# Retention queries and keys in the Strassen form, and their T4 (with that of nine other units) made by an accumulating load

## The chip, the cores and the metric

The kernel runs on one core of a Trainium2 chip. The metric is the device time of one execution in microseconds, the median of three. The engines are named as the profile names them: PE is TensorE (matmuls), DVE is VectorE, ACT is ScalarE, POOL is GpSimd, and SP issues plain DMAs.

## The reference, cut to what matters

One decoder block on 512 tokens of width 1024, all in float32. Only the input projection and what hangs on it bears on this change.

```
h = rmsnorm(x, norm1_w);  proj = h @ w_in
rq, rk, rv, rg, mq, mk, mv, ga, gb = split(proj)      # widths 512 512 1024 1024 512 512 512 1024 1024
rq, rk = rotary(rq), rotary(rk) * 128**-0.5           # 4 heads of 128
ret = silu(rg) * groupnorm(retention(rq, rk, rv));  a = ret @ w_ret_out
b = moba_attention(rmsnorm(mq), rmsnorm(mk), mv) @ w_moba_out
x = x + (sigmoid(ga) * a + sigmoid(gb) * b) @ w_o
x = x + (silu(rmsnorm(x) @ w_gate) * (rmsnorm(x) @ w_up)) @ w_down
```

## The kernel before, in words

All weights lie in one DRAM array, `wall`, as chunks of 128x1024 floats (512 KB), in the order in which they are used. A float32 product is made of three float32r products: each weight chunk is split into a high half `wh` (a cast on ACT, L407) and a low half `wl` (a subtraction on DVE), and `mm3` runs high x high, high x low and low x high. So each 128x1024 piece costs a load, a cast on ACT and a subtraction on DVE. Every engine call recorded by the pacing helper has line 218, so tiles tell more than lines.

Work comes in units. A unit in the Strassen form (`wino_unit`) takes four weight quarters B11, B12, B21, B22 of one chunk each (a wide one takes two) and makes seven products of 24 matmuls of 256 columns: B11, T1, T2, B21, B22, T3, T4, where T1 is a sum of the stored chunks of B12 and B11, T3 of B22 and B12, T2 = T1 + B22 and T4 = T2 + B21 (the signs aside). T1 and T3 are made by loads alone: SP loads one chunk (L332), and GpSimd adds the other by an accumulating DMA (L334). T2 is made by DVE in place (`raw<-raw,raw`, 128x1024). T4 was made in the same way by DVE, except in wide units with two chunks to a quarter (`w_o`, most of `w_ffn_down`), where an accumulating DMA issued right behind T2's low half does it (L371). T4's product runs late: in a Strassen unit that follows, behind that unit's T1 product. A unit's results leave PSUM through `Quarters`: three ACT copies (a plain one at L859, two negated ones at L862 and L865) and two DVE subtractions of 128x512 into a tile `qb`, and then the unit's own work.

A unit in the plain feature form (`feat_blocks`) takes its weights as they are: four chunks, four pieces, 192 matmuls of 256 columns.

`ORDER` sets the units: mv, rg0, rk0, rv0, gb0, rk1, rv1, rg1, gb1, b0, b1, ga0, a0, ga1, a1, then w_o and the feed-forward part. (rg: retention gate, rk: retention queries and keys of two heads, rv: values, ga and gb: branch gates, a and b: branch outputs.) `WRQ` says whether rk0 and rk1 run in the Strassen form; before, they don't.

Between groups of matmuls a second stream runs from a list `bg`: one step per 24 matmuls in the feature form, one per 12 in the Strassen form. First come 38 attention steps (scores on PE; on DVE a row maximum `mx`, its scaled negative `nb`, a reciprocal `rl`, the scaling of `p`; on ACT the exponential `p` and copies `pt` out of PSUM), spread over rg0, rk0, rv0 and gb0, then retention scores, retention values with their statistics (`bs`, `mvs`), and the gate `qa<-qa,r_y,sg` in halves of 256 columns. rk's own results go through rotary on DVE: `rot`, three multiplications and an addition for each of four results, then a cast on ACT and a low half on DVE.

All eight PSUM banks and the 47 slots of 128x1024 in SBUF are shared by every kind of tile, so a new tile waits for the last reader of the slot it gets. Each engine runs its queue in the order in which the program wrote it; nothing overtakes.

The raw chunks in flight are limited: one that has been split frees its slot, and that issues the next load. At most three pieces, at times four, are split and not yet used up.

Of the kernel before, what the change touches and what calls it, by code (L numbers as in the profile page):

```python
# [40 lines left out]
OEXTRA = 5  # L41
FEXTRA = -2
ORDER = (("rg", 0), ("rk", 0), ("rv", 0), ("gb", 0), ("rk", 1), ("rv", 1), ("rg", 1), ("gb", 1), ("b", 0), ("b", 1), ("ga", 0), ("a", 0), ("ga", 1), ("a", 1))
WRQ = (0, 0)
RLAG = (1, 2, 3)
SLAG = (1, 1, 1)
ROT = 1
# [11 lines left out]
HLAG = 1  # L59
LLAG = 1  # L60
CHUNKS = (6, 6, 6, 4)
T4DMA = ("X2",)


K_ID, K_ONE, K_NEG, K_TRI, K_GM, K_GN, K_COS, K_SIN = 0, 128, 256, 384, 512, 528, 544, 1056
# [15 lines left out]
def weight_plan():  # L81
# [19 lines left out]
    def wino(name1, col1, name2, col2, order=NORMAL):  # L101
        quarters = ((name1, col1, 0), (name2, col2, 0), (name2, col2, 4), (name1, col1, 4))
        units.append(("W", [(n, (k0 + k) * P, c + i * P) for n, c, k0 in quarters for i in (0, 1) for k in range(4)],
                      order))
# [3 lines left out]
    def cols(col):  # L108
        units.append(("X", ("w_in", halves, col, 256), NORMAL))
# [3 lines left out]
    for name, i in ORDER:  # L113
        if name == "rg":
            cols(C_RG + 512 * i)
        elif name == "rv":
            cols(C_RV + 512 * i)
        elif name == "rk" and WRQ[i]:
            wino("w_in", C_RQ + 256 * i, "w_in", C_RK + 256 * i)
# [21 lines left out]
def quarter_parts(unit):  # L141

    if unit[0] == "W":
        return [1024]
    _, rows, _, half = unit[1]
    n = len(rows[0]) * half
    return [min(1024, n - i) for i in range(0, n, 1024)]


def unit_chunks(unit):  # L150
    return 4 * len(quarter_parts(unit)) if unit[0] in "WX" else 2
# [14 lines left out]
def hybrid_block(ctx: ExitStack, tc: tile.TileContext, wall, xin, xtok, n2, cin, out):  # L166
# [107 lines left out]
    chunk, chunk_of, width, t4dma = 0, {}, {}, set()  # L274
    for u, unit in enumerate(plan):
        chunk_of[u] = chunk
        if unit[0] in "WX":
            ws = quarter_parts(unit)
            order = unit[2].split()
            if f"{unit[0]}{len(ws)}" in T4DMA:  # L280
                t4dma.add(u)
            for j, n in enumerate(ws):
                for q in ("B11", "B21", "B22", "T1", "T2", "T3", "T4"):
                    width[u, (q, j)] = n
            if unit[2] == PLAIN:
                loads += [(u, (q, 0), [chunk + c]) for q, c in (("B11", 0), ("B21", 3), ("B12", 1), ("B22", 2))]
                porder += [(u, (q, 0)) for q in order]
                for q in order:
                    width[u, (q, 0)] = 1024
                chunk += 4  # L290
                continue
            for q, cs in WLOADN if order.index("T1") < order.index("B21") else WLOAD:
                loads += [(u, (q, j), [chunk + c * len(ws) + j for c in cs]) for j in range(len(ws))]
            rest = False
            for q in order:
                if q == "/":
                    rest = True
                elif q[0] == "*":
                    for _ in range(int(q[1:])):
                        porder += left.pop(0) if left else []  # L300
                else:
                    x = [(u, (q[:3].rstrip("w"), j)) for j in range(len(ws))]
                    if rest:
                        left.append(x)
                    else:
                        porder += x
        else:
            loads += [(u, i, [chunk + i]) for i in range(2)]
            porder += sum(left, [])
            left = []  # L310
            if u >= STARTERS:
                porder += [(u, i) for i in range(2)]
            for i in range(2):
                width[u, i] = 1024
        chunk += unit_chunks(unit)
# [217 lines left out]
    def two(x):  # L533
        return x.rearrange("p (u c) -> p u c", u=2)
# [78 lines left out]
    for k in range(KT):  # L613
        if k % 2 == 0:
            hf[k // 2] = big(f"hf{k}")
        f = two(hf[k // 2])[:, k % 2]
# [166 lines left out]
    def wino_unit(w, ev, hooks={}):  # L783

        u = cur[0]
        cur[0] += 1
        order = plan[u][2].split()
        wide = plan[u][0] == "X" and plan[u][1][3] == 512
        banks = {}

        def bank(b):
            if b not in banks:
                z = zbank if b == "Z" else main_ps()
                banks[b] = [z, main_ps()] if wide else z
            return banks[b]

        def third(x):
            ev.c22(x)
            if "T4w" in order:
                ev.u3(x)  # L800

        def first(x):
            ev.p1(*([x, bank("Z")] if seed else [x]))

        whole = "T4w" in order
        seed = not wide and order[1] != "B21"
        table = {"B11": ("X", "A11", True, False, first), "T1": ("Y", "S1", True, False, ev.p5),
                 "T2": ("X", "S2", False, False, ev.u2), "B21": ("Z", "A12", not seed, True, ev.c11),
                 "B22": ("Y", "S4", False, True, ev.c12), "T3": ("X", "S3", False, whole, third),
                 "T4": ("X", "A22", False, True, ev.c21),  # L810
                 "T4w": ("W", "A22", True, True, getattr(ev, "c21w", None))}

        def run(q):
            b, m, start, stop, out = table[q]
            wino_prod(w, u, bank(b), m, q.rstrip("w"), start, stop, out)

        rest = False
        for q in order:
            if q == "/":
                rest = True  # L820
            elif q[0] == "*":
                for _ in range(int(q[1:])):
                    wino_finish()
            elif rest:
                wpend.append(lambda q=q: run(q))
            else:
                run(q)
                if q in hooks:
                    hooks[q]()
# [310 lines left out]
    def rot_out(h0):  # L1140
        def f(r, c, x):

            a, b = halves(nm("rot"))
            hf = RDK // 2
            if h0 is None:
                c, h = c
                V.tensor_tensor(a, x, cosT, ALU.mult)
                V.tensor_tensor(b[:hf], x[hf:], sinT[hf:], ALU.mult)
                V.tensor_tensor(b[hf:], x[:hf], sinT[:hf], ALU.mult)
                V.tensor_tensor(a, a, b, ALU.add)  # L1150
                (rqT, rkT)[c][h] = split(f"r{c}_{h}", a, None, SLAG[1])
                return
            cos, sin = (y[:, r * 256:(r + 1) * 256].unsqueeze(1).to_broadcast([P, 2, 256]) for y in (cosT, sinT))
            V.tensor_tensor(two(a), two(x), cos, ALU.mult)
            V.tensor_tensor(two(b)[:hf], two(x)[hf:], sin[hf:], ALU.mult)
            V.tensor_tensor(two(b)[hf:], two(x)[:hf], sin[:hf], ALU.mult)
            V.tensor_tensor(a, a, b, ALU.add)
            if (c, h0) not in rT:
                H, L = big(f"rH{c}_{h0}", F32R), big(f"rL{c}_{h0}", F32R)
                rT[c, h0] = H, L  # L1160
                for i in (0, 1):
                    s = slice(i * 512, (i + 1) * 512)
                    (rqT, rkT)[c][h0 + i] = Two(H[:, s], L[:, s])
            H, L = (two(y)[:, :, r * 256:(r + 1) * 256] for y in rT[c, h0])
            later(ROT, lambda: A.copy(H, two(a)))
            later(ROT + 1, lambda: V.tensor_tensor(L, two(a), H.bitcast(F32), ALU.subtract))
        return f
# [141 lines left out]
    def rk_unit(n):  # L1309
        h = 2 * n  # L1310
        if WRQ[n]:
            wino_unit(hW, Quarters(rot_out(h)))
# [415 lines left out]
```

## Time and profile before

| | |
|---|---|
| median of three executions | 801.82 us (799.88 to 802.16) |
| the profiled execution | 800.78 us, of which the span of the trace is 798.7 us |
| PE busy | 782.8 us (98%) |
| DVE busy | 648.9 us (81%) |
| ACT busy | 439.8 us (55%) |
| granted clock of PE | 0.997 over the whole |

The span runs from the first to the last instruction. Busy PE counts time in which a matmul was under way; with 98% busy, nearly each microsecond less of matmul is a microsecond less of time, unless PE then waits for something else.

### The profile page before, as it was taken

To read this page: it belongs to the slowest core of one execution; us is meant where nothing else is said; L and a number is where in the kernel's file an instruction comes from. 1 tells how busy PE (TensorE), PEld (TensorE's weight loads), DVE (VectorE), ACT (ScalarE), POOL (GpSimd) and SP (SyncE) were. 2 spreads that over 40 slices of the span, in tenths; PEclk is the share of its full clock that TensorE was granted. 3 is DMA by queue.
4 is the path that set the end of the run, shared out by engine and by line. 5 is a ranking of instruction groups with operands and counts; after the bars stand their busy time and mean duration, and the time that the engine had idled before them with its cause. 6 is when DMAs were issued, how large, how long until landed. Compare 5 with 4: busy or idle time off the path is not lost.

```text
span 798.7 us, 13670 instructions
## 1 busy us (share of the span) xinstructions
PE 782.8 (98%) x5398; PEld 722.8 (90%) x5398; DVE 648.9 (81%) x978; ACT 439.8 (55%) x722; POOL 64.1 (8%) x84
## 2 busy tenths in 40 slices
PE   6999999999999999999999999999999999999998
PEld 5889998889899998998988798988999899988996
DVE  7789877977799588877578989879887978889877
ACT  8457764757337458653445565544555455645541
POOL 0004000000000000000001000011101110111000
PEclk9999999999999999999999999999999999999999
DMA  9843352334426547371799705579836893689502
GB/s 330 230 113 80 115 128 50 106 80 133 125 67 179 133 136 182 106 185 56 230 353 246 170 1 132 126 193 291 231 102 180 221 287 111 150 213 294 136 1 106
DMA packets 38080, 125.95 MB, mean 158 GB/s; under 512 B 4224, under 2 KB 4480, under 8 KB 38016
## 3 DMA queue, kind: packets, MB, share of 16 engines
q1 hardware_dynamic: 28800, 93.88, 33.8%
q0 software_dynamic: 9216, 31.20, 22.5%
q8 instruction: 42, 0.69, 0.3%
q14 instruction: 22, 0.18, 0.1%
HBM read 122.97 MB, written 2.10 MB: 157 GB/s over the span
## 4 chain that ended last, share of the span: by engine, by line
PE 84%; DVE 8%; ACT 4%; issue 2%; DMA 2%; POOL 0%; SPq 0%; DVEq 0%; ACTq 0%; POOLq 0%
PE pm L218 76%; PE ps L218 8%; DVE wl L218 2%; ACT wh L407 2%; DMA raw<-wall 2%; DVE xr L218 1%; DVE raw L218 1%; DVE ws L218 1%; DVE h L218 1%; DVE fb L218 1%; DVE gs L218 1%; DVE gsl L218 0%; ACT f L1508 0%; ACT h L1496 0%; DVE xn L218 0%
## 5 line engine op out<-in xcount | busy, mean ns | idle before, releaser
L218 DVE TENSOR_TENSOR wl<-raw,wh 128x1024 fp32r<-128x1024 f32 x203 | 245.1, 1220 | 44.7 <-ACT wh L407 34.7
L407 ACT CAST wh<-raw 128x1024 fp32r<-128x1024 f32 (+1 forms) x224 | 219.5, 1006 | 67.6 <-DVE raw L218 47.5
L218 PE MATMUL pm<-h,wh 128*128 128x256 f32 x1248 | 227.3, 285 | 3.3 <-ACT h L1496 1.3
L218 PEld LDWEIGHTS pm<-h,wh 128*128 128x128 f32 x1248 | 196.3, 193 | 4.8 <-ACT h L1496 1.5
L218 PE MATMUL pm<-h,wl 128*128 128x256 f32 x624 | 177.2, 284 | 0.0
L218 PEld LDWEIGHTS pm<-h,wl 128*128 128x128 f32 x624 | 120.5, 193 | 0.0
L334 POOL DMA_DIRECT2D raw<-wall x56 | 49.6, 898 | 633.3 <-DMA raw<-wall 153.3
L218 PE MATMUL pm<-hA,wh 128*128 128x256 f32 x448 | 83.2, 286 | 1.8 <-DVE qb L218 1.8
L218 PEld LDWEIGHTS pm<-hA,wh 128*128 128x128 f32 x448 | 70.1, 192 | 3.0 <-DVE qb L218 2.0
L218 PE MATMUL pm<-wh,hA 128*128 128x256 f32 (+1 forms) x304 | 69.1, 310 | 0.0
L218 PE MATMUL pm<-wh,hS 128*128 128x256 f32 x320 | 63.1, 287 | 0.4 <-ACT pm L859 0.4
L218 PE MATMUL pm<-hA,wl 128*128 128x256 f32 x224 | 63.4, 283 | 0.0
L218 DVE TENSOR_TENSOR raw<-raw,raw 128x1024 f32<-128x1024 f32 (+1 forms) x48 | 57.0, 1189 | 0.8
L218 PEld LDWEIGHTS pm<-wh,hA 128*128 128x128 f32 x304 | 51.0, 191 | 2.4
L218 PEld LDWEIGHTS pm<-wh,hS 128*128 128x128 f32 x320 | 51.7, 191 | 0.9 <-ACT pm L859 0.6
L218 DVE TENSOR_TENSOR xr<-xr,pm 128x512 f32<-128x512 f32 x74 | 47.1, 681 | 1.3 <-PE pm L218 1.3
L218 PE MATMUL pm<-hS,wh 128*128 128x256 f32 x256 | 47.4, 285 | 0.0
L218 PE MATMUL pm<-wl,hA 128*128 128x256 f32 (+1 forms) x152 | 46.5, 306 | 0.0
L218 PE MATMUL pm<-wl,hS 128*128 128x256 f32 x160 | 45.3, 283 | 0.0
L218 PEld LDWEIGHTS pm<-hA,wl 128*128 128x128 f32 x224 | 42.8, 191 | 0.0
L218 PE MATMUL pm<-wh,gsh 128*128 128x512 f32 x112 | 39.9, 391 | 0.2
L218 PEld LDWEIGHTS pm<-hS,wh 128*128 128x128 f32 x256 | 40.0, 192 | 0.1
(254 smaller groups left out, 1397.9 us busy)
## 6 DMA issues: line engine op xcount, KB each, us to landing
raw<-wall SPq DMA_DIRECT2D x153, 512.0 KB, 4.6
raw<-wall POOLq DMA_DIRECT2D x55, 512.0 KB, 6.9
raw<-wall SPq DMA_DIRECT2D x23, 256.0 KB, 4.8
raw<-wall POOLq DMA_DIRECT2D x9, 256.0 KB, 6.7
xr<-xtok SPq DMA_DIRECT2D x4, 512.0 KB, 7.7
out<-xr SPq DMA_DIRECT2D x8, 256.0 KB, 2.1
x<-xin SPq DMA_DIRECT2D x7, 256.0 KB, 5.4
cs<-cin SPq DMA_DIRECT2D x1, 512.0 KB, 5.5
```

Of the source, the lines that this page charges most:

```text
L218: return f(out, *args, **kw)
L334: nc.gpsimd.dma_start(t[:, s], wall[c, :, s], accum_op=ALU.add)
L407: A.copy(h, src)
```

## The change

Three edits go together. `WRQ = (1, 1)` puts rk0 and rk1 into the Strassen form: 168 matmuls of 256 columns each instead of 192, seven pieces to cast and split instead of four, a T2 sum on DVE, three copies on ACT and two subtractions on DVE to take the quarters out of PSUM, and 14 steps of the second stream instead of 10 (both with the two of the T4 product that runs inside the unit). `T4CHUNKS = 52` makes T4 by an accumulating load wherever the unit's first chunk is below 52: in mv, rg0, rk0, rv0, gb0, rk1, rv1, rg1, gb1 and ga0. In the eight of these that were in the Strassen form before, a DVE sum of 128x1024 goes and a GpSimd DMA comes. The wide units keep theirs, so the rest of the program has its old order.

```
-WRQ = (0, 0)
+WRQ = (1, 1)
...
-T4DMA = ("X2",)
+T4CHUNKS = 52
...
         if unit[0] in "WX":
             ws = quarter_parts(unit)
             order = unit[2].split()
-            if f"{unit[0]}{len(ws)}" in T4DMA:
+            if len(ws) > 1 or chunk < T4CHUNKS:
                 t4dma.add(u)
```

In the built program PE has 5310 matmuls instead of 5358, GpSimd issues 14 more DMAs (four for T1 and T3 of the two rk units, ten for T4), SP two more. From ga0's T4 on, every engine has the same order as before.

Place one, VectorE at the end of rk0. Before: the T2 sum of rv0 (`raw_1162`), one rotary group, attention, and T2's low half.

```order
L218 TENSOR_REDUCE mx<-ps_1617 128x2
L218 SCALAR_TENSOR_TENSOR nb<-mx,qs 128x2
L218 RECIPROCAL rl<-l 128x2
L218 TENSOR_SCALAR p_1628<-p_1628,rl 128x128 x2
L218 TENSOR_TENSOR raw_1162<-raw_1162,raw_1246 128x1024
L218 TENSOR_TENSOR r_1_1631<-rot_1590,r_1_1631 128x512
L218 TENSOR_TENSOR rot_1683<-pm_1577,cs 128x512
L218 TENSOR_TENSOR rot_1683<-pm_1577,cs 64x512 x2
L218 TENSOR_TENSOR rot_1683<-rot_1683 128x512
L218 TENSOR_REDUCE mx<-ps_1697 128x2
L218 SCALAR_TENSOR_TENSOR nb<-mx,qs 128x2
L218 TENSOR_TENSOR wl_1725<-raw_1162,wh_1688 128x1024
```

Now, at the place where PE stands before the transposes of `p_1746` (T4's product of rk0 is half done):

```order
L218 TENSOR_TENSOR rL_0_1678<-rot_1672,rH_0_1677 128x2x256
L218 RECIPROCAL rl<-l 128x1
L218 TENSOR_SCALAR p_1692<-p_1692,rl 128x384
L218 TENSOR_TENSOR rot_1764<-qb_1214,cs 128x512
L218 TENSOR_TENSOR rot_1764<-qb_1214,cs 64x512 x2
L218 TENSOR_TENSOR rot_1764<-rot_1764 128x512
L218 TENSOR_TENSOR raw_1358<-raw_1358,raw_1437 128x1024
L218 TENSOR_REDUCE mx<-ps_1770 128x1
L218 SCALAR_TENSOR_TENSOR nb<-mx,qs 128x1
L218 RECIPROCAL rl<-l 128x1
L218 TENSOR_SCALAR p_1746<-p_1746,rl 128x512
```

Two of the three rotary groups ahead of this place now read `qb`, which a DVE subtraction made, and rv0's T2 sum has moved to between the last of them and the maximum of `ps_1770`, with a whole attention step behind it.

ScalarE at the same place. Before: exponentials with one cast between them.

```order
L1035 ACTIVATE p_1856,l<-ps_1845,nb,qs 128x512
L407 CAST wh_1873<-raw_1400 128x1024
L1035 ACTIVATE p_1886,l<-ps_1875,nb,qs 128x512
L865 ACTIVATE qb_1669<-pm_1670 128x512
L1067 COPY pt_1763<-ps_1907 128x2x128
L1072 COPY pt_1765<-ps_1907 128x128
```

Now: behind the exponential of `ps_1770` stand the cast of a rotary result, the copy that seeds a bank of rv0, the cast of rv0's T2, and only then the copies that free the bank `ps_1802`.

```order
L1035 ACTIVATE p_1781,l<-ps_1770,nb,qs 128x512
L1165 CAST rH_0_1677<-rot_1764 128x2x256
L859 COPY pm_218<-pm_1707 128x512
L407 CAST wh_1800<-raw_1358 128x1024
L1067 COPY pt_1642<-ps_1802 128x2x128
L1072 COPY pt_1644<-ps_1802 128x128
```

PE's next scores, `ps_1876`, take the bank that `ps_1802` leaves, so they have moved behind all six of these rows.

Place two, VectorE from rk1 to rv1. Before, rv1's T2 sum (`raw_2378`) and its low half stand among the rotary groups of rk1, early, since a feature unit uses few pieces:

```order
L218 TENSOR_TENSOR raw_2378<-raw_2378,raw_2431 128x1024
L218 TENSOR_TENSOR r_2_2726<-rot_2705,r_2_2726 128x512
L218 TENSOR_TENSOR rot_2768<-pm_2691,cs 128x512
L218 TENSOR_TENSOR rot_2768<-pm_2691,cs 64x512 x2
L218 TENSOR_TENSOR rot_2768<-rot_2768 128x512
L218 TENSOR_TENSOR wl_2813<-raw_2378,wh_2785 128x1024
L218 TENSOR_TENSOR raw_2378<-raw_2378,raw_2503 128x1024
```

Now (`raw_2613` is rv1's T1, then its T2, `wl_2909` the low half that rv1's T2 product needs):

```order
L218 TENSOR_TENSOR rot_2861<-qb_2466,cs 128x512
L218 TENSOR_TENSOR rot_2861<-qb_2466,cs 64x512 x2
L218 TENSOR_TENSOR rot_2861<-rot_2861 128x512
L218 SCALAR_TENSOR_TENSOR qa_836<-qa_836,r_y,sg_2845 128x256 x2
L218 TENSOR_TENSOR raw_2613<-raw_2613,raw_2648 128x1024
L218 SCALAR_TENSOR_TENSOR qb_837<-qb_837,r_y,sg_2869 128x256 x2
L218 TENSOR_TENSOR rL_2_2822<-rot_2861,rH_2_2821 128x2x256
L218 SCALAR_TENSOR_TENSOR qb_837<-qb_837,r_y,sg_2891 128x256 x2
L218 TENSOR_TENSOR wl_2909<-raw_2613,wh_2889 128x1024
L218 TENSOR_TENSOR wl_2927<-raw_2680,wh_2912 128x1024
```

The gates and the rotary of rk1 have moved ahead of rv1's T2, and T4's sum, which stood behind its low half, is gone.

## Rows read from the trace of the kernel before

**Rows 1.** The page: share of the chain that ended last, by engine.

```profile
PE 84%; DVE 8%; ACT 4%; issue 2%; DMA 2%; POOL 0%; SPq 0%; DVEq 0%; ACTq 0%; POOLq 0%
```

**Rows 2.** Windows view, rk0, rv0, rk1, rv1, a stretch: busy times, clock, DMA.

```profile
101.69:136.55 34.86, 34.86 (x279) 32.19 (x278) 27.24 (x58) 17.68 (x44) 1.73 (x2) 1.00 0.39 92
136.55:166.35 29.80, 29.80 (x228) 26.36 (x227) 25.63 (x54) 21.20 (x55) 0.86 (x1) 1.00 0.31 89
...
196.87:229.53 32.66, 30.86 (x254) 30.52 (x252) 25.75 (x52) 13.79 (x25) 1.72 (x2) 1.00 0.43 112
229.53:250.29 20.76, 20.76 (x176) 20.76 (x174) 17.63 (x29) 13.24 (x22) 1.72 (x2) 1.00 0.52 153
...
131.00:151.00 20.00, 20.00 (x153) 17.67 (x153) 18.31 (x35) 10.21 (x29) 0.86 (x1) 1.00 0.09 28
```

**Rows 3.** The chain, pieces in order: start, us, engine and tile, instructions.

```profile
81.15 5.76 PE pm L218 x48
...
108.58 0.33 PE ps L218 x3
...
120.08 2.90 PE ps L218 x20
...
133.88 0.81 PE ps L218 x7
...
211.57 2.52 PE ps L218 x21
```

**Rows 4.** Timeline around TensorE's idle time in rk1 (in brackets: idle before).

```profile
206.62 0.68 DVE L218 TENSOR_TENSOR qb<-qa,pm 128x512 f32<-128x512 f32 x1
...
207.35 0.51 PE L218 MATMUL pm<-hA,wh 128*128 128x256 f32 x2 [1.80 <-DVE qb L218]
```

**Rows 5.** Timeline of VectorE: start, duration, operation, count.

```profile
109.45 2.09 DVE L218 TENSOR_TENSOR rot<-pm,cs 128x512 f32<-128x512 f32 x3
111.58 0.69 DVE L218 TENSOR_TENSOR rot<-rot 128x512 f32<-128x512 f32 x1
112.19 1.22 DVE L218 TENSOR_TENSOR wl<-raw,wh 128x1024 fp32r<-128x1024 f32 x1
113.32 0.68 DVE L218 TENSOR_REDUCE mx<-ps 128x2 f32<-128x512 f32 x1
...
135.11 0.15 DVE L218 RECIPROCAL rl<-l 128x1 f32<-128x1 f32 x1
...
135.70 1.22 DVE L218 TENSOR_TENSOR wl<-raw,wh 128x1024 fp32r<-128x1024 f32 x1
...
215.48 0.43 DVE L218 BATCH_NORM_STATS2 bs<-ps 128x6 f32<-128x256 f32 x1
...
216.57 0.66 DVE L218 TENSOR_TENSOR r<-rot,r 128x512 fp32r<-128x512 f32 x1
...
243.96 0.88 DVE L218 SCALAR_TENSOR_TENSOR qa<-qa,r_y,sg 128x256 f32<-128x256 f32 x2 [0.43 <-ACT sg L1268]
```

**Rows 6.** Timeline of ScalarE: one row of each operation of the chain.

```profile
128.26 0.78 ACT L1035 ACTIVATE p<-ps,nb,qs 128x512 f32<-128x512 f32 x1 [1.10 <-DVE nb L218]
...
129.03 0.61 ACT L478 CAST r<-rot 128x512 fp32r<-128x512 f32 x1
...
134.51 0.27 ACT L1072 COPY pt<-ps 128x128 f32<-128x128 f32 x1
...
237.32 1.05 ACT L407 CAST wh<-raw 128x1024 fp32r<-128x1024 f32 x1
238.27 0.59 ACT L859 COPY pm<-pm 128x512 f32<-128x512 f32 x1
```

**Rows 7.** Tile raw and DMA issues, 56 to 310 us: GpSimd's accumulating loads.

```profile
L334 POOL DMA_DIRECT2D raw<-wall x12: 862/862/865, 63.9 to 302.4; - x12
...
raw<-wall POOLq DMA_DIRECT2D x12, 512.0 KB, 6.3
```

**Rows 8.** Timeline of ScalarE in the feed-forward part: a cast that waited.

```profile
636.52 1.06 ACT L407 CAST wh<-raw 128x1024 fp32r<-128x1024 f32 x1 [3.19 <-DMA raw<-wall]
```


## The prediction

> **What bounds the kernel now.** I read the page's chain first: TensorE holds 84% of it [rows 1]. Then the timeline of TensorE: from rg0 to the end of ga1 it idles just once, 1.80 us in rk1 [rows 4]. So in the stages that the change touches a matmul less is time less, as long as the engines that feed TensorE keep up. How near they are to not keeping up is in the windows of the units: VectorE is busy 27.24 of 34.86 us in rk0, 25.63 of 29.80 in rv0 (86%), 25.75 of 32.66 in rk1 and 17.63 of 20.76 in rv1, and TensorE waits for none of it but the 1.80 [rows 2]. VectorE thus has some 15% to give away, and the question is what the change asks of it, and where.
>
> **What is removed on TensorE.** A Strassen unit has 168 matmuls of 256 columns where the feature unit has 192: 24 less for rk0 and 24 for rk1. The chain has a piece of just that size, 48 matmuls in 5.76 us, 0.12 each [rows 3]. So -5.76 us, if nothing new waits.
>
> **The idle time in rk1.** TensorE waits at 207.35 for a subtraction into `qb` [rows 4]. That subtraction stands on VectorE behind a low half of the retention scores, and that behind a cast on ScalarE into a slot which TensorE's T4 product of gb0 was still reading. It comes from which slot a new tile gets, in gb0's T4, which shares its time with retention scores. In the changed program retention scores start earlier (attention is over by the end of rv0), and I find no subtraction at that place which TensorE would need at once. I count the 1.80 as gone; its bounds are 0 and 1.80.
>
> **What VectorE gets.** For each rk unit: three low halves more, a T2 sum and two subtractions of 128x512. For eight other units the T4 sum goes. The low half and the sum of 128x1024 follow each other by 1.13 to 1.22 us (112.19 to 113.32), 128x512 by 0.61 (111.58 to 112.19) [rows 5]. So 2 x (4 x 1.15 + 2 x 0.61) = +11.6 against 8 x 1.15 = -9.2: nearly nothing over the whole. But the gain lies in mv, rg0, gb0, rg1, gb1 and ga0, while the load lies in rk0 and rk1, where the rotary is too, and rk0 now runs 14 steps of attention instead of 10. A mean says nothing here; I add up VectorE's queue between two points at which it is tied to TensorE.
>
> **Place one, rk0's T4.** In the changed program 57 VectorE instructions stand between the maximum of a fresh score group in rk0 (which can't start before TensorE has made it) and the scaling of `p_1746`, which TensorE's next transposes read. Their prices: five of 128x1024 at 1.15, 5.75; three rotary groups, 2.74 each by 109.45 to 112.19 with PSUM as source, and 2.44 if a source in SBUF made all four run at 0.61, I take 2.6, 7.8; six of 128x512 at 0.61, 3.7; eight attention steps at 1.33 (maximum 0.65 with its negative 0.09, reciprocal and scaling 0.59 by 135.11 to 135.70), 10.6 [rows 5]. Sum 27.85. TensorE has 144 products, 17.3, and 66 small matmuls in that time. In before one full period of attention has 60 of these, in eight pieces of the chain from 108.58 to 133.88 that sum to 8.53 [rows 3]; 66 make 9.4, and up to 10.2 since more of them are wide. I take 9.8, so 27.1 in all. With 0.3 for the hand-overs at both ends (estimate from 206.62 + 0.68 to 207.35 [rows 4], and the tail of a matmul) TensorE waits 1.0 there.
>
> Behind that wait is a second one. `ps_1876` needs the bank that ScalarE frees with its sixth row behind the maximum of `ps_1770`: exponential 0.77 (128.26 to 129.03), cast 0.5 to 0.6, seeding copy 0.5 to 0.59, cast of T2 0.95 (237.32 to 238.27), two copies of 0.27 [rows 6]: 3.25. The negative maximum is done 0.75 ahead of the end of the first wait, so the bank is free 3.25 - 0.75 + 0.1 = 2.6 behind it, and TensorE has 0.35 of transposes to do meanwhile. Place one costs 1.0 + 2.2 = 3.2; between 2.0 and 4.0 by the bounds of rotary and attention.
>
> **Place two, rv1's T2.** Here 38 VectorE instructions stand between the statistics of a fresh retention value group in rk1 and `wl_2909`, the low half that rv1's T2 product needs with its second matmul. Eight of the statistics, 1.09 for four (215.48 to 216.57), 2.2; five of 128x1024, 5.75; three rotary groups, 7.8; five of 128x512, 3.05; eight halves of the gate at 0.40 to 0.44, 3.3 [rows 5]. Sum 22.1. TensorE has 133 products, 16.0, and 21 matmuls of retention values, 2.52 [rows 3]: 18.5. With the hand-overs TensorE waits 3.8 there (3.2 to 4.4). In before the same T2 was split among the rotary groups of rk1, early, since a feature unit asks for four pieces in the time in which a Strassen unit asks for seven.
>
> The same sums over the program of before give no place at which VectorE's queue is longer than TensorE's; that agrees with the trace, whose one wait in this stage comes by way of ScalarE.
>
> **What costs nothing.** ScalarE gets three casts and three copies for each rk unit, some 4.5 us beside 17.68 of 34.86 and 13.79 of 32.66 [rows 2]; outside place one its queue stays shorter than TensorE's. GpSimd issues 14 DMAs more, 0.86 us each, landing 6.3 us after [rows 7]; it has little else to do here. T4's chunk is loaded behind T2's low half and cast five pieces later, 5 x 24 x 0.12 = 14.4 us, against 7.2 for issue and landing, so 7 us are over; before a feature unit (b0, a0) it is cast three pieces later, 8.6 us, and TensorE needs it some products after that. The cover is this distance; without it ScalarE's cast waits and all behind it in its queue.
>
> On GpSimd's DMAs the Trainium skill has a rule that speaks against the change (SBUF — State Buffer, Who interferes with whom): GpSimd can't write its descriptors while VectorE holds the port pair that they share. The same section says that a two-input operation on tensors takes only the pair's read interface, and infers that descriptor writing needs the other. The trace agrees with that: 862 ns at least, in the median 862 and at most 865 for the issues of this stage [rows 7]. So the sum gets nothing from it; by the rule's blocked case a T4 load would come late, which is the last rival.
>
> **Sum.** -5.76 - 1.80 + 3.2 + 3.8 = -0.56 us on the profiled execution's 800.78. The median of the runs is 1.04 above that execution, so the same difference from 801.82: 801.2 us. What a measurement of this kernel can tell from no change is about 0.3%, 2.4 us.
>
> **The rivals.**
> - Both waits appear, as summed: 801.2, own range 799.6 to 803.2. Chance 0.48.
> - One of the two doesn't appear, because a wait ahead of it has already moved TensorE back or my price of the rotary is high: -7.56 + 3.8 or + 3.2, 797.5 to 798.1. For it speaks that each is a difference of two large sums. Chance 0.20.
> - Neither appears, VectorE's spare 15% take it all: -7.56, 794.3. Against it: both queues start from a result that TensorE has just made, so working ahead can't shorten them. Chance 0.08.
> - Slower: VectorE can't run its two queues without gaps. In the tightest 20 us of before that left TensorE alone it was busy 18.31, 92% [rows 2], with waits for ScalarE between. At 92% the two sums, 49.9 together, become 4.3 longer, 805.6. It is slower by more than 0.3% from 94% downward (3.0 more). Against it: a queue that is behind finds its inputs ready. Chance 0.17.
> - The accumulating loads come late. In the feed-forward part a cast waited 3.19 for such a load [rows 8]; the same once in rk1, behind which VectorE is already late, gives 804.4. Chance 0.07.
>
> The range 797.2 to 805.6 leaves out the third and about half of the fourth. Faster: the second and third and the lower edge of the first, 0.30. Slower: the fourth and half of the last, 0.21. Same: 0.49.
>
> **What would show it.** Right: 48 matmuls less, no idle time at gb0's T4, and two new groups of idle time of TensorE, one before the transposes and scores at rk0's T4 (released by VectorE's `p` and ScalarE's `pt`), one before rv1's T2 product (released by `wl`), 3 to 4 us each, with VectorE at 95% or more ahead of both. From ga0 on the stages should be as long as before. Wrong: TensorE without idle time at one of the places, VectorE with gaps released by ScalarE inside the queues, casts that wait for DMAs between 60 and 310 us, or a new wait that I haven't named.

## The result, and the profile after

The changed kernel takes 806.76 us in the median of four executions (805.73 to 808.91), the kernel before 801.02 us on the same chip: ratio 1.0079, 95% interval 1.0063 to 1.0095. It is slower by about 6 us, outside the predicted range. The profiled execution took 805.73 us with a span of 804.0 us, 5.3 us more than before.

The page of after first (its line of TensorE, the granted clock in 40 slices, and the chain's shares). PE has 5350 records where the page of before has 5398, the 48 matmuls of the change (both are 40 above the counts of the built programs). Against [rows 1] the chain holds less of PE and more of DVE and DMA, and two slices of the clock line, each 20.1 us long, show an 8: those that hold 150 and 245 us.

```profile
PE 779.5 (97%) x5350; PEld 719.0 (89%) x5350; DVE 651.1 (81%) x982; ACT 448.0 (56%) x734; POOL 76.4 (9%) x98
...
PEclk9999999899998999999999999999999999999999
...
PE 70%; DVE 14%; issue 6%; ACT 5%; DMA 5%; POOL 0%; SPq 0%; DVEq 0%; POOLq 0%; ACTq 0%
```

The windows of rk0, rv0, rk1 and rv1, which answer to [rows 2] (the column behind POOL is the granted clock). In rk0 and rk1 TensorE is busy without a break. The loss is in rv0 and rv1, where TensorE is idle for 4.49 and 4.09 us and the mean clock is 0.92 and 0.87. (rk0's T4 product now runs inside rv0, rk1's inside rv1, and the steps of the second stream lie elsewhere too, so the lengths of the units can't be compared one by one.)

```profile
100.32:136.08 35.76, 35.76 (x278) 31.51 (x277) 27.34 (x60) 23.94 (x63) 2.62 (x3) 1.00 0.46 111
136.08:176.31 40.23, 35.74 (x256) 31.38 (x255) 34.76 (x71) 25.50 (x61) 2.62 (x3) 0.92 0.43 111
...
202.16:230.24 28.08, 28.08 (x236) 28.08 (x235) 23.87 (x44) 15.19 (x24) 2.59 (x3) 1.00 0.62 167
230.24:257.48 27.24, 23.15 (x170) 22.75 (x169) 23.47 (x34) 13.66 (x21) 2.62 (x3) 0.87 0.59 150
```

TensorE's timeline at place one (start, duration, tiles, in brackets the idle time before and its releaser). The transposes of `p` wait 2.75 us, the scores behind them 1.28 us for the bank that a `pt` copy frees. Behind that, it is 0.64 us from the start of one group of three matmuls of 256 columns to the start of the next (154.93 to 155.57).

```profile
143.55 0.36 PE L218 MATMUL ps<-mk3h,mq 128*128 128x256 f32 x1 [0.46 <-DVE moT L218]
...
150.21 1.11 PE L218 MATMUL ps<-cst,p 128*128 128x128 f32 x4 [2.75 <-ACT p L1035]
152.61 0.80 PE L218 MATMUL ps<-mk3h,mq 128*128 128x512 f32 x1 [1.28 <-ACT pt L1072]
...
154.93 0.63 PE L218 MATMUL pm<-hA,wh 128*128 128x256 f32 x2
...
155.57 0.63 PE L218 MATMUL pm<-hA,wh 128*128 128x256 f32 x2
```

And at place two, ahead of rv1's T2 product: 2.01 us for `wh`, one matmul, 2.08 us for `wl`, and again 0.64 us for three matmuls (243.90 to 244.54).

```profile
241.05 0.38 PE L218 MATMUL pm<-wh,hS 128*128 128x256 f32 x1 [2.01 <-ACT wh L407]
243.52 0.58 PE L218 MATMUL pm<-wl,hS 128*128 128x256 f32 x1 [2.08 <-DVE wl L218]
243.90 0.63 PE L218 MATMUL pm<-wh,hS 128*128 128x256 f32 x2
...
244.54 0.63 PE L218 MATMUL pm<-wh,hS 128*128 128x256 f32 x2
```

The two stretches that the prediction added up can be measured, since the start and the end of each are in the trace. At place one the 57 VectorE instructions run from the maximum at 118.62 to the end of the scaling of `p` at 149.79, at place two the 38 from 220.72 to the end of the low half at 243.46 (one window each; the first busy time is TensorE's, the third VectorE's):

```profile
118.62:149.79 31.17, 28.38 (x218) 25.35 (x217) 27.59 (x58) 14.48 (x38) 0.86 (x1) 1.00 0.29 81
220.72:243.46 22.74, 18.71 (x154) 18.30 (x152) 22.15 (x39) 11.24 (x20) 0.86 (x1) 0.97 0.55 146
```

At place two VectorE is busy nearly throughout, 22.15 of 22.74 us. At place one it has 27.59 us of work in a stretch of 31.17: it stood still twice for ScalarE, for 2.80 us together, the rest in short breaks, and from 132.54 on it is busy nearly throughout.

```profile
125.36 0.17 DVE L218 RECIPROCAL rl<-l 128x2 f32<-128x2 f32 x1 [0.96 <-ACT p L1035]
132.54 0.69 DVE L218 TENSOR_TENSOR rL<-rot,rH 128x512 fp32r<-128x512 f32 x1 [1.84 <-ACT rH L1165]
```

In the windows around the waits (columns as in [rows 2]) VectorE is busy 3.90 of 4.00 us just ahead of the end of the first wait, and behind the waits of each place the granted clock is 0.50, the lower of TensorE's two levels, 1.2 GHz. It is at 1.00 again from 157 us, and at 0.98 over the 3 us from 249 us.

```profile
146.00:150.00 4.00, 1.46 (x13) 1.26 (x11) 3.90 (x8) 0.71 (x2) 0.00 (x0) 1.00 0.35 131
...
153.00:157.00 4.00, 4.00 (x17) 3.38 (x17) 3.14 (x7) 3.32 (x11) 1.75 (x2) 0.50 0.46 60
157.00:160.00 3.00, 3.00 (x26) 2.84 (x25) 2.18 (x6) 2.63 (x9) 0.00 (x0) 1.00 1.09 216
...
243.00:247.00 4.00, 3.48 (x16) 3.48 (x17) 3.94 (x6) 1.17 (x2) 1.76 (x2) 0.50 0.38 54
...
249.00:252.00 3.00, 3.00 (x27) 3.00 (x26) 2.43 (x3) 1.39 (x3) 0.00 (x0) 0.98 1.05 231
```

The idle time at gb0's T4 [rows 4] is gone. One wait is new and stands in none of the sums, 1.33 us at 313.21. The chain of after leads to it from an accumulating load of GpSimd, the one for gb1's T4: issued at 293.82, landed 7.87 us later (the slowest of the nine T4 loads up to there, whose median is 5.8), the cast at 301.77, for which ScalarE had then waited 3.14 us, and then VectorE, late from there on, up to `qb`.

```profile
293.82 7.87 DMA raw<-wall
...
301.77 1.05 ACT wh L407
...
312.55 0.61 DVE qb L218
...
313.21 1.80 PE pm L218 x13
```

What the lower clock costs is read off the spacing: 0.213 us from one matmul of 256 columns to the next (a third of 0.64) instead of 0.12. At place two the 26 matmuls from 243.52 to 249.1 are 26 x 0.093 = 2.4 us longer. At place one twelve of 256 columns take 2.70 us (154.15 to 156.85), 1.26 more than 12 x 0.12, and three scores of 512 columns start 0.43 apart instead of 0.24, 0.6 more: 1.8. The kernel before had such a stretch too, late, behind its wait of 1.28 us at 457.69: 21 matmuls in 4 us where the next 4 us have 36, some 1.6 us.

```profile
459.00:463.00 4.00, 4.00 (x21) 3.81 (x20) 3.44 (x6) 3.59 (x8) 0.00 (x0) 0.57 0.00 0
463.00:467.00 4.00, 4.00 (x36) 4.00 (x35) 3.52 (x11) 3.31 (x6) 0.00 (x0) 1.00 0.00 0
```

In after there is none at that point. The account of the profiled executions: -5.76 (matmuls) - 1.80 (old wait) + 0.46 + 4.03 (place one) + 4.09 (place two) + 1.8 + 2.4 (lower clock behind them) - 1.6 (before's own stretch) + 1.33 (the load) = +4.95, against +5.3 measured. The start of the program was 1.0 us shorter in this execution of after, so some 1.4 us stay unplaced.

### The profile page after: what moved, and what is told of

Its sections match the earlier page's. It is cut to its first block, busy times and chain, and to the rows that moved or that the text cites. A ratio compares the mean times of both kernels' runs of the same rounds, so it can differ in the third digit from the quotient of the medians.

```text
span 804.0 us, 13623 instructions
## 1 busy us (share of the span) xinstructions
PE 779.5 (97%) x5350; PEld 719.0 (89%) x5350; DVE 651.1 (81%) x982; ACT 448.0 (56%) x734; POOL 76.4 (9%) x98
## 3 DMA queue, kind: packets, MB, share of 16 engines
q0 software_dynamic: 11232, 38.54, 27.1%
## 4 chain that ended last, share of the span: by engine, by line
PE 70%; DVE 14%; issue 6%; ACT 5%; DMA 5%; POOL 0%; SPq 0%; DVEq 0%; POOLq 0%; ACTq 0%
PE pm L218 65%; PE ps L218 5%; DMA raw<-wall 5%; DVE wl L218 3%; ACT wh L407 2%; DVE rot L218 2%; DVE xr L218 1%; DVE raw L218 1%; DVE h L218 1%; DVE gs L218 1%; DVE fb L218 1%; DVE ws L218 1%; DVE xn L218 1%; DVE mx L218 1%; ACT p L1035 0%
## 5 line engine op out<-in xcount | busy, mean ns | idle before, releaser
L218 DVE TENSOR_TENSOR wl<-raw,wh 128x1024 fp32r<-128x1024 f32 x209 | 252.1, 1220 | 49.0 <-ACT wh L407 39.7
L407 ACT CAST wh<-raw 128x1024 fp32r<-128x1024 f32 (+1 forms) x230 | 225.6, 1007 | 73.9 <-DVE raw L218 40.0
L334 POOL DMA_DIRECT2D raw<-wall x60 | 55.3, 948 | 471.5 <-DMA raw<-wall 137.3
L218 PE MATMUL pm<-hS,wh 128*128 128x256 f32 x384 | 71.4, 286 | 0.0
L218 PEld LDWEIGHTS pm<-hS,wh 128*128 128x128 f32 x384 | 59.9, 192 | 0.6 <-issue 0.3
L218 PE MATMUL pm<-hA,wh 128*128 128x256 f32 x288 | 55.0, 290 | 1.3 <-DVE qb L218 1.3
L218 PE MATMUL pm<-hS,wl 128*128 128x256 f32 x192 | 54.3, 283 | 0.0
L218 DVE TENSOR_TENSOR raw<-raw,raw 128x1024 f32<-128x1024 f32 (+1 forms) x42 | 49.6, 1182 | 0.5
L218 PEld LDWEIGHTS pm<-hA,wh 128*128 128x128 f32 x288 | 46.0, 195 | 2.1 <-DVE qb L218 1.8
L218 PE MATMUL pm<-hA,wl 128*128 128x256 f32 x144 | 41.2, 286 | 0.0
```

The costliest lines, as they stand in the source:

```text
L218: return f(out, *args, **kw)
L334: nc.gpsimd.dma_start(t[:, s], wall[c, :, s], accum_op=ALU.add)
L407: A.copy(h, src)
```

## The experiments

The theory (A): VectorE's two long queues make the two waits, and each wait is paid twice, since the granted clock falls behind it. The rival (B): the accumulating loads come late and make the loss. Each ratio is against the kernel before on the same chip.

**The Strassen form alone**, without the new accumulating loads.

```
 (kernel before)
-WRQ = (0, 0)
+WRQ = (1, 1)
```

> The kernel before with retention queries and keys in the Strassen form; every T4 sum stays where it was, on VectorE. Theory A (each of the two units brings its own wait of TensorE, and behind the wait a stretch at the half granted clock: after shows 2.75 + 1.28 + 0.46 us of waits and 150.3 to 157.0 us at 0.50 in the first place, 2.01 + 2.08 us and 242.3 to 249.1 at 0.50 in the second): both places again, with the T4 sums on VectorE at 1.15 us each in front of them, and no wait near 313: 806 to 809 us. Theory B (the loss comes from the accumulating loads, which reach ScalarE's casts late: 3.59, 2.09 and 3.14 us in after): the units alone give their 48 matmuls, 5.76 us, and at most one of the waits: 795 to 799 us.

808.45 us, ratio 1.0089 (1.0060 to 1.0118). B falls: without the loads the loss is as large. The waits are those of after (2.76 + 1.39 and 2.19 + 2.08 us), with the lower clock behind both places:

```profile
150.99 1.01 PE L218 MATMUL ps<-cst,p 128*128 128x128 f32 x4 [2.76 <-ACT p L1035]
...
244.60 0.58 PE L218 MATMUL pm<-wl,hS 128*128 128x256 f32 x1 [2.08 <-DVE wl L218]
```

**The loads alone.**

```
 (changed kernel)
-WRQ = (1, 1)
+WRQ = (0, 0)
```

> The changed kernel with retention queries and keys back as a feature unit, so only T4 by accumulating loads is left of the change. Theory A (the two Strassen units bring the waits): no wait at the two places, no stretch at half clock before 440 us, 799 to 802 us, the same as before within 0.3%. Theory B (late loads): the 3 to 5 us of loss are here, 804 us or more, with ScalarE's casts waiting 2 to 4 us for loads, and TensorE waiting for these casts.

803.62 us, ratio 1.0040 (1.0024 to 1.0056). Not the 799 to 802 of theory A: beside the feature units the loads cost 3 us. But not in B's way either: in rv0 no cast waits for a load. TensorE waits for attention, 1.76 + 0.65 us:

```profile
147.77 1.07 PE L218 MATMUL ps<-pt,mv 128*64 128x512 f32 x2 [1.76 <-ACT p L1035]
149.49 1.07 PE L218 MATMUL ps<-pt,mv 128*64 128x512 f32 x4 [0.65 <-ACT pt L1067]
```

The exponential waits for the negative maximum `nb`, which starts at 146.26 on VectorE, 2.0 us later than in before (144.29), though TensorE is 0.8 us ahead of before here. VectorE became late further up: a low half (`wl`) waited 3.45 us for TensorE, and the maximum behind it starts at 130.47:

```profile
129.33 1.23 DVE L218 TENSOR_TENSOR wl<-raw,wh 128x1024 fp32r<-128x1024 f32 x1 [3.45 <-PE pm L218]
130.47 0.69 DVE L218 TENSOR_REDUCE mx<-ps 128x1 f32<-128x512 f32 x1
...
146.26 0.16 DVE L218 SCALAR_TENSOR_TENSOR nb<-mx,qs 128x2 f32<-128x2 f32 x1
```

In before the low half ahead of that maximum didn't wait, and the maximum starts 3.2 us earlier:

```profile
125.63 1.22 DVE L218 TENSOR_TENSOR wl<-raw,wh 128x1024 fp32r<-128x1024 f32 x1
127.28 0.69 DVE L218 TENSOR_REDUCE mx<-ps 128x1 f32<-128x512 f32 x1 [0.43 <-PE ps L218]
...
144.29 0.16 DVE L218 SCALAR_TENSOR_TENSOR nb<-mx,qs 128x2 f32<-128x2 f32 x1
```

So without its T4 sums VectorE's queue has the pieces in another order: the next T2 sum, too, stands earlier (at 132.95 us, in before at 139.11). That this order costs the 2.4 us is read from the rows, and no run here isolates it. The profile also has a longer wait near 460 us (2.36 instead of 1.28 us), at a place that no edit touches.

**Only the second pair of heads in the Strassen form.**

```
 (changed kernel)
-WRQ = (1, 1)
+WRQ = (0, 1)
```

> The changed kernel with only the second pair of heads (rk1) in the Strassen form; rk0 is a feature unit again. Theory A: the first place is gone with its half clock, the second stays: 801.0 - 2.88 (24 matmuls) + 4.1 of wait + 2.4 at half clock = 804.6 us; between 802.8, if the 1.80 us wait of before at gb0's T4 is gone, and 805.9, if it stays and the 1.33 us at 313 comes again. Theory B: the loads decide, so the time is near that of the kernel that has the loads alone, less 2.88. A rival to A, that the two places hang together (the second wait is there because the first has shifted the work): no wait before rv1's T2, 797 to 799 us.

801.70 us (799.68 to 804.71, ten executions), ratio 1.0018 (1.0001 to 1.0035), below the 802.8 to 805.9 of theory A. rk0 is a feature unit again, and the wait is that of the run before (1.76 + 0.65 at 147.56). Place two waits on its own, so it doesn't hang on the first, but less, 2.08 + 0.57 us, and in the profiled execution, one of the fastest (799.95 us), the clock stayed at 1.00:

```profile
240.98 0.39 PE L218 MATMUL pm<-wl,hS 128*128 128x256 f32 x1 [2.08 <-DVE wl L218]
...
240.00:249.00 9.00, 7.45 (x60) 7.25 (x61) 8.94 (x13) 5.82 (x11) 1.75 (x2) 1.00 0.66 127
```

**Work without effect during the waits**, first try: matmuls with weights of zeros, added to an open sum. (In the cut, numbers stand for the constants that hold them, and the line that fills `zerob` with zeros is left out.)

```
+    def fill(bank, n):
+        for _ in range(n):
+            T.matmul(two(bank)[:, :, :P], lhsT=zerob, rhs=identb.unsqueeze(1).to_broadcast([P, 2, P]),
+                     start=False, stop=False, skip_group_check=True)
...
+        if (u, q) == (10, "T2"):
+            fill(bank, 30)
         for j, n in enumerate(ws):
             pc = piece(u, (q, j))
             for i in (0, 1):
+                if (u, q, i) == (6, "T4", 1):
+                    fill(bank, 22)
```

> The changed kernel in which TensorE is given work without effect while it waits: 22 matmuls of 256 columns with weights of zeros, added to the open sum of rk0's T4 (2.6 us) ahead of the transposes that wait for p, and 30 (3.6 us) ahead of rv1's T2 product. The output stays the same. Theory A with the clock (the granted clock falls because TensorE stood still, and that costs 2.3 us in the first and 2.4 us in the second place): waits for the same work end at the same time, the clock stays at 1.00 in both places, 802.1 us. Rival (the clock falls for another reason, or the stretch at half clock costs nothing because VectorE is late there in any case): 806.8 us, as after, or more if the added matmuls are in the way.

806.54 us, ratio 1.0069 (1.0043 to 1.0095): no gain in the sum, but the 22 matmuls had landed behind the wait they were to fill, at the lower clock, as 4.01 us of extra work. Place two is the test, and there the clock held:

```profile
154.48 4.01 PE L220 MATMUL pm<-identb,zerob 128*128 128x256 bf16 x22
...
241.00:247.00 6.00, 4.45 (x39) 3.79 (x37) 5.84 (x11) 4.33 (x8) 0.00 (x0) 1.00 0.27 87
```

**The same with the first group ahead of the wait.**

```
-                if (u, q, i) == (6, "T4", 1):
-                    fill(bank, 22)
...
+                if (u, q, i) == (6, "T4", 0):
+                    fill(bank, 22)
                 run_bg(1)
```

(and 24 instead of 30 at place two)

> As the first kernel with work without effect, but the 22 matmuls of zeros stand ahead of the transposes that wait (there they came behind them and ran 22 times 0.17 us on top), and the second group has 24 instead of 30. Theory A (the granted clock falls because TensorE stands still): the clock is at 1.00 through both places, the waits for p, pt and wl end as they did, so 806.8 - 2.3 - 2.4 = 802.1 us, and 800.8 if the 1.33 us at 313 is gone again. Rival (the clock falls in the first place in any case, or VectorE is late by as much and takes the gain back): 805 us or more.

802.43 us, ratio 1.0029 (1.0014 to 1.0043): with 46 useless matmuls more the kernel is 4 us faster than the changed one. The waits still end where VectorE and ScalarE end them, but at place two the clock is 1.00 throughout. At place one the wait for `pt`, 1.74 us, could not be filled, and a shorter stretch at the lower clock stands behind it:

```profile
152.33 0.50 PE L220 MATMUL ps<-mk3h,mq 128*128 128x512 f32 x1 [1.74 <-ACT pt L1085]
...
153.00:157.00 4.00, 4.00 (x22) 3.72 (x21) 2.87 (x7) 3.32 (x11) 1.75 (x2) 0.58 0.55 71
...
243.79 0.39 PE L220 MATMUL pm<-wl,hS 128*128 128x256 f32 x1 [1.44 <-DVE wl L220]
...
243.00:246.00 3.00, 2.21 (x18) 2.21 (x19) 2.99 (x4) 1.44 (x3) 1.73 (x2) 1.00 0.19 18
```

The 1.33 us at 313 are missing here too, so the clock's share of the 4 us is 2.5 to 3 (an estimate, by the two profiles). The Trainium skill (TensorE: Matmul & The Clock Gate, part 1) says that the clock is set by how busy the array has been of late; at place two these two runs agree, since useless work was enough to hold it.

**The gates behind rv1's T2.** Eight more empty steps ahead of the first four gate steps.

```
 (changed kernel)
-RGATE = (2, 0)
+RGATE = (10, 0)
```

> The changed kernel with eight more empty steps ahead of the first four gate steps, so that all eight gate halves of VectorE (0.40 to 0.44 us each, 3.3 us) stand behind rv1's T2 instead of in front of it. If VectorE's queue makes the second wait: TensorE waits 4.1 - 3.3 = 0.8 us there, the clock does not fall, 806.8 - 3.3 - 2.4 = 801.1 us. Rival (ScalarE's cast of the same sum or the load behind it holds the place, so the wait stays over 2 us and the clock falls): 804 to 807 us.

804.51 us, ratio 1.0047 (1.0034 to 1.0060): 2.6 us better than the change. The wait falls from 4.09 to 1.85 us, not to 0.8: T2's sum, its cast and its low half still follow each other. And the clock fell behind it all the same, for a shorter time:

```profile
239.78 0.39 PE L218 MATMUL pm<-wh,hS 128*128 128x256 f32 x1 [0.97 <-ACT wh L407]
241.05 0.39 PE L218 MATMUL pm<-wl,hS 128*128 128x256 f32 x1 [0.88 <-DVE wl L218]
...
241.50:245.00 3.50, 3.50 (x21) 3.50 (x20) 3.44 (x6) 0.72 (x2) 1.54 (x2) 0.57 0.59 95
```

**Fewer steps of attention in rk0.**

```
 (changed kernel)
+SKIP = [(6, q, i) for q in ("B21", "B22", "T3") for i in (0, 1)]
...
-                run_bg(1)
+                if (u, q, i) not in SKIP:
+                    run_bg(1)
```

> The changed kernel in which six of rk0's fourteen pieces issue no step of attention, eight instead of fourteen; the steps follow in rv0 and gb0. If the fourteen steps made the first wait (27.85 us of VectorE's instructions against 27.1 of TensorE's): eight steps less in a unit are some 4 us less for VectorE, the first place has at most 2 us of waits, no fall of the clock, and the second place stays as in after: 806.8 - 2.5 to 4.5 - 2.3 = 800.0 to 802.0 us. Rival (attention that ends later makes a new wait in gb0 or rk1 of the same size): 805 us or more.

800.84 us (797.42 to 804.26, ten executions), ratio 1.0016 (0.9999 to 1.0032), in the expected range. In the profile, which is of the fastest of the ten, place one has 0.92 + 0.70 us of waits instead of 4.03 and keeps its clock. So fourteen steps in place of eight made 2.4 us of the waits at place one. Place two has 0.54 + 2.08 us, less than in after, and the clock fell behind it.

**Both edits together.**

```
 (changed kernel)
-RGATE = (2, 0)
+RGATE = (10, 0)
...
+SKIP = [(6, q, i) for q in ("B21", "B22", "T3") for i in (0, 1)]
```

> The two previous edits together: fewer steps of attention in rk0, the gates behind rv1's T2. If the two places are independent and the clock falls in neither, the matmuls show through: 801.0 - 5.76 - 1.80 + 2.0 (what is left of both waits) = 795.4, between 794 and 798 us, faster than before by more than 0.3%. Rival (one of the waits goes elsewhere, or the accumulating loads bring their own 3 us as they did alone): 799 us or more.

797.47 us, ratio 0.9965 (0.9952 to 0.9979): faster than both kernels, at the upper end of what was expected. What is left: 0.91 + 0.70 us at place one, 1.63 + 0.88 at place two, and one stretch at the lower clock.

```profile
140.79 0.43 PE L219 MATMUL ps<-cst,p 128*128 128x128 f32 x2 [0.91 <-DVE p L219]
...
235.42 0.39 PE L219 MATMUL pm<-wh,hS 128*128 128x256 f32 x1 [1.63 <-ACT wh L408]
236.69 0.58 PE L219 MATMUL pm<-wl,hS 128*128 128x256 f32 x1 [0.88 <-DVE wl L219]
...
236.70:240.00 3.30, 3.30 (x17) 3.30 (x17) 3.24 (x5) 1.05 (x2) 1.75 (x2) 0.55 0.48 55
```

**The same without the new loads.**

```
 (the kernel of the run before)
-T4CHUNKS = 52
+T4CHUNKS = 0
```

> The version with fewer steps and later gates, but every T4 sum of these units back on VectorE and no accumulating load for them. Three theories of what the loads are worth there. They relieve VectorE where it is late (nine sums of 1.15 us leave it, two of them in front of the two places): 2 to 5 us slower than with the loads, 799.5 to 802.5 us. They are worth nothing, since the sums lie where VectorE has room: 797.5 us. They cost their 3 us as they did beside the feature units: 794.5 us.

797.97 us, ratio 0.9970 (0.9954 to 0.9987), the same as with them. The second theory holds: the accumulating loads are worth nothing that can be measured, here as beside the plain change (1.0079 with them, 1.0089 without; in both pairs the intervals overlap).

**The changed kernel a second time.**

> The changed kernel once more, for a second profile of it. If waits and stretches at half clock belong to the program: waits of 2.75 and 1.28 us in the first and 2.0 and 2.1 us in the second place, the granted clock at 0.50 for about 7 us behind the start of both, and the 1.33 us at 313 again. If a part of it is chance, that part is missing or elsewhere.

805.32 us, span 803.5. Waits and lower clock at both places come again to within 0.04 us; the wait at 313 does not, its cast waited 1.91 us for the load instead of 3.14. In its place a stretch at the lower clock follows the wait of 1.20 us at 462.41, as in before and not in the first profile. Those two parts differ between two executions of one program.

```profile
150.03 1.11 PE L218 MATMUL ps<-cst,p 128*128 128x128 f32 x4 [2.75 <-ACT p L1035]
...
243.26 0.58 PE L218 MATMUL pm<-wl,hS 128*128 128x256 f32 x1 [2.08 <-DVE wl L218]
...
242.00:248.00 6.00, 4.74 (x22) 4.75 (x23) 5.94 (x8) 2.81 (x5) 1.75 (x2) 0.50 0.47 83
```

The first pair of heads alone in the Strassen form was not tried.

## Why the prediction was wrong

**The matmuls and the old wait** were right: 48 less, and no idle time at gb0's T4.

**Place two** was right in mechanism and size. VectorE's queue was busy 22.15 us for 22.1 in the sum, in a stretch of 22.74, TensorE 18.71 for 18.5, and the wait was 4.09 for 3.8. The eight gate halves behind T2 took away 2.2 us of it.

**Place one** was right in place and kind, and its total, 0.46 + 4.03 us for 3.2, is nearly right only because errors offset each other, which is luck. The prices held: 27.59 us of VectorE's work for 27.85. But the sum took this queue to run without gaps, and it stood still for ScalarE for 2.80 us, so that it took 31.17 us. TensorE had 28.38 us of work beside it instead of 27.1, and stood 0.46 us on attention's `moT`, which was not foreseen. So the first wait was 2.75 us for 1.0; by the profile its last 0.4 us were ScalarE's exponential, behind `p`. The bank came free 2.8 us behind `p`, for 2.6 in the sum, but more of that lay under the first wait and under transposes that took 1.1 us, while the clock fell, instead of 0.35: the second wait was 1.28 for 2.2. Eight steps of attention in rk0 instead of fourteen took away 2.4 us of the two.

**The step that failed is the sum itself**: "-5.76 - 1.80 + 3.2 + 3.8" counts a wait at its own length and puts what follows it at nothing. The lower clock behind the two waits cost another 4.2 us, net 2.6 in the profiled execution since before's own late stretch was missing there. The trace of before held the price, in the windows around 461 us shown above; I had looked at the clock only as a mean of 0.997. With 7.0 of waits corrected to 8.6, the clock's 2.6 and the load's 1.33, the predicted -0.56 becomes +4.95; the other 1.4 us of the profiled difference stay open.

**The rivals.** The slower rival, a VectorE that can't run its two queues without gaps, gave nearly the time, 805.6, and came true by half: VectorE was busy 89% of the first stretch and 97% of the second. It counted 4.3 us of gaps in both; the gaps released by ScalarE were 2.80 us, at place one alone, and most of the rest of the loss was the clock, which stood in no rival. The late loads (804.4) did occur, in one of the two profiles, with 1.33 us, and at the place that the prediction named as the shorter cover: the T4 load ahead of a feature unit. For its cover the prediction counted 8.6 us; ScalarE was there 4.8 us after the issue. That GpSimd might be kept from its issues by VectorE (the Trainium skill, SBUF — State Buffer, Who interferes with whom) did not show: all nine issues of T4 loads up to 294 us took 862 to 865 ns. Issues of T1 and T3 loads that stand directly behind another issue show up to 1571 ns. The late load was slow in landing.

**What costs nothing** was right for ScalarE outside place one and wrong for the loads: beside the feature units they go with another order on VectorE and cost 3 us, and the 9.2 us of sums that they take off VectorE are worth nothing.

## What to carry to other kernels

Where a helper engine is 85% busy, less work for TensorE is only a gain if the helper's queue between two hand-overs stays the shorter one; sum that queue, with its own waits for a third engine, and then move what need not stand in it (attention steps, gates), as here a loss of 0.8% became a gain of 0.35%. A wait of TensorE costs its length and, behind it, often a stretch in which each matmul takes nearly twice as long: look for such a stretch in the windows of the trace that you have, and price new waits with it. Work taken off an engine at places where nobody waits for it was worth nothing here, and can change the order for the worse.

## What the runs showed of the hardware

The length of a wait does not decide alone whether the granted clock falls. It stayed at 1.00 behind 1.80 us in before [rows 4], behind 1.76 + 0.65 in two runs and behind 2.08 + 0.57 in one; it fell behind 0.97 + 0.88 with later gates, behind 0.54 + 2.08 in the run with fewer steps, behind the 1.74 us that could not be filled, and behind every unfilled wait of 4 us. Near 460 us, at a place that no edit touches, TensorE waits in all twelve profiles. Behind 2.33 to 2.36 us, in four of them, the clock fell each time; behind 1.2 to 1.5 us it fell in three (before among them) and held in five (after among them). What else decides was not settled. With fewer steps, the ten executions of one program run from 797.42 us at a mean granted clock of 0.998 to 804.26 us at 0.991, so one profile does not stand for all of them. Useless matmuls during a wait kept the clock up at place two in both runs that tried.
